# Two token blocks in alternation: a reordering inside the products by token of a two-layer encoder trunk on one Trainium2 core

## The chip, the cores and the metric

The kernel runs on one core of one Trainium2 chip. Four engines do the work that matters here. PE (TensorE) multiplies: a matmul reads a stationary operand of up to 128x128 and streams a moving operand past it, and it sums into a bank of PSUM (128 partitions x 512 floats). ACT (ScalarE) and DVE (VectorE) read and write SBUF and PSUM, and empty the banks. POOL (GpSimd) does almost nothing here. SP (SyncE) issues the loads and stores. Each engine works through its own queue strictly in order and waits on semaphores for what other engines produce.

The metric is the device time of one launch in microseconds (us). The kernel before was timed in three runs: the median is 1181.94 us, the lowest 1181.73 us, the highest 1183.77 us.

## The reference

The reference is a trunk of two layers over 512 tokens of width 1024, in fp32, with a memory of 256 tokens.

```
for i in range(DEPTH):                                   # DEPTH = 2
    h = rms_norm(x, attn_norm[i])
    if i % 2 == 0:  proj = h @ w_in_diff;  mix = diff_attention(q, k, v, ...)
    else:           proj = h @ w_in_gla;   mix = gla_attention(q, k, v, r, gate_low, ...)
    cross = memory_cross_attention(mem_q, mem, mem_norm[i], w_mem_kv[i], mem_qk_norm[i])
    x = x + concatenate([mix, cross]) @ w_out[i]
    h = rms_norm(x, ffn_norm[i])
    x = x + conv_ffn(h, w_up[i], conv_w[i], conv_b[i], w_down[i])
```

Layer 0 has differential attention with 6 heads: each head computes two softmaxes over 512 keys and subtracts them. Layer 1 has gated linear attention with 4 heads. In both layers 4 heads attend to the memory, whose keys and values are `rms_norm(mem) @ w_mem_kv[i]`, with one such product for each layer. The root mean square is taken over the whole width of a token, so its factor can be multiplied in after the product, one number for each token (row).

## The kernel before, in words

**Products.** Every fp32 product is made of three matmuls on operands that are split in a high and a low part: high x high, high x low and low x high. The weights arrive as raw fp32 tiles of 128x1024 by DMA (tile `raw`, three buffers). ACT casts each to its high part (`whi`, L205), and DVE subtracts to get the low part (`wlo`, L208); there are six buffers of each (`WB = 6`).

**Products by token.** `gemm` is the function that the change touches. A block of 128 tokens is the stationary operand, and the weights stream past it, up to 512 columns wide, so each block of tokens has its result in one bank of PSUM named `mm`, of which there are two. The inner width of 1024 is eight `k` of 128, and a unit of work is one block with two `k`: six matmuls. A weight tile of 128x1024 holds two `k` at 512 columns, so a unit uses one pair of tiles `whi`, `wlo`. With four blocks of tokens a `gemm` is 16 units; with the memory's 256 tokens it has two blocks and is 8 units. When a block has all eight `k`, `evac` empties its bank on ACT (two copies of 128x256 with a factor for each row, in most of them). `freed` is called by the last block after each `k`: when a pair of weight tiles has had its last use, it issues the cast and the subtraction of the next raw tile into the buffers and the load of a further one. Before the change block 0 takes all its `k`, then block 1, and so on.

Eleven calls of `gemm` are in the kernel. In layer 0: `vm0` (values of heads 0 and 1, and the memory queries), `qk1`, `kv0` (keys and values of the memory for layer 0), `v1`, `qk2` and `kv1` (the memory for layer 1). In layer 1: `gm1` (272 columns wide) and `g0` to `g4`. The two of the memory have `nb = 2`, the others `nb = 4`.

**The hook of kv0.** The memory's factor `r_mem` is computed by `token_rsqrt` (L370): four matmuls with a vector of ones (L373) sum the squares for each token into a bank `lg`, and then `rsqrt` runs Ln and Exp on ACT (L195, L196) and a Newton step on DVE (`newton`, L181 to L183). `gemm` calls this as its `hook` when block 0 has its last `k`, just ahead of the first `evac`. Only `kv0` and `gm1` have a hook; `kv1` reuses `r_mem`. Both evacuations of `kv0` (L499 for the keys, L500 for the values) multiply by `r_mem`.

**What sets the order.** PE's order is written out by hand. The units of `gemm` are put in a queue `F` (class `Filler`), and the attention of layer 0 goes through steps `t` = 0 to 20, each of which issues its own transposes, logits and value products and, between them, as many units of `F` as fit in a budget of microseconds (`FILL`, chosen with `STEPS`). A step has one unit of a head's attention: `logits(t)` (L650 on PE, L655 on DVE, L658 on ACT, L663 to L666 on DVE), `turn(t-1)` (transposes at L174, copied by ACT at L676) and `values(t-2)` (L688). `PREPARE` tells at which step a head's queries and keys are transposed (8 transposes into two banks `tp`, each copied by ACT at L617 to `qT` and `kT`); head `h` has its logits at steps 3h to 3h+2. `FINISH` tells at which step a head's output is transposed. The orders of ACT, DVE, POOL and SP are chosen by the framework's planner from the program's order and its own estimates of time.

**Layer 1** uses the same filler: the units of `g0` to `g4` run between the steps of the memory attention (L539 logits, L542 maximum, L546 exponential, L550 scaling, L559 copies) and of the gated heads (L926, L934). `g0` is emptied by two copies at L806, of 128x384 and 128x128.

The lines around the change stand in the kernel as follows.

Of the kernel before, what the change touches and what calls it, by code (L numbers as in the profile page):

```python
# [22 lines left out]
KT = D // 128  # L23
# [11 lines left out]

TOGETHER = ((2, 0), (1,), (3,))

PREPARE, FINISH = {5: 2, 7: 3, 11: 4, 13: 5}, {7: 0, 11: 1, 12: 2, 15: 3, 18: 4}
K8 = tuple(range(KT))
C4 = tuple(range(4))  # L40

# [92 lines left out]
def trunk(ctx, tc, head_d, x_t, mem_t, wpack, cols_a_d, cols_d, conv_d, gate_d, rel_bias, diff_lambda, consts, onehot, out):  # L134
# [12 lines left out]
    def bank(tag):  # L147
        return ps.tile([128, 512], F32, name=f"ps_{tag}", tag=tag)
# [12 lines left out]
    def blk(b, w=128):  # L161
        return slice(w * b, w * b + w)
# [84 lines left out]
    def weights(key, by_block=False):  # L247
        i = used[0]
        assert plan[i][0] == key, (plan[i][0], key)
        limit = first_of[i] + WB if by_block else first_of[min(i + 2, len(plan))]  # L250
        while done[0] < min(max(limit, first_of[i + 1]), len(order)):
            make_block()
        used[0] += 1
        parts, made[i] = made[i], None
        return parts

    def freed(i, k):
        if k in [sum(len(b[2]) for b in blocks[i][:j + 1]) - 1 for j in range(len(blocks[i]))] and done[0] < len(order):
            make_block()
# [6 lines left out]
    F = Filler()  # L266

    def gemm(sh, sl, nb, key, w, evac, hook=None):
        got, open_ = [], {}

        piece = [q[0] for q in plan].index(key)

        def unit(b, k0, k1):
            if not got:
                got.extend(weights(key, True))
            if k0 == 0:
                open_[b] = bank("mm")[:, :w]
            p = open_[b]
            for k in range(k0, k1):
                hi, lo = got[k]  # L280
                mm(p, sh[k][:, blk(b)], hi, start=k == 0, stop=False)  # L281
                mm(p, sh[k][:, blk(b)], lo, start=False, stop=False)  # L282
                mm(p, sl[k][:, blk(b)], hi, start=False, stop=k == KT - 1)  # L283
                if b == nb - 1:
                    freed(piece, k)
            if k1 == KT:
                if hook is not None and b == 0:
                    hook()
                evac(b, open_.pop(b))
        for b in range(nb):  # L290
            for k in range(0, KT, 2):
                F.add(6 * w / 2370.0, lambda b=b, k=k: unit(b, k, k + 2))


    def product(p, parts, n, pairs, ids=None):
# [90 lines left out]
    with tc.tile_pool(name="ini", bufs=1) as ip, tc.manual_schedule(engines={E.Activation, E.DVE, E.Pool, E.SP}):  # L386
# [53 lines left out]
        for k in range(KT):  # L440
# [22 lines left out]
            for b, i, t in todo:  # L463
                xp, w = terms[i]
# [18 lines left out]
    def mem_kv(l):  # L483
# [18 lines left out]
        def keys(tag="lg"):  # L502
            F.need(f"kv{l}")
            p = bank(tag)
            for hp in range(2):
                for b in range(2):
                    transpose(p[:, 256 * hp + 128 * b:256 * hp + 128 * b + 128], km[0][:, b, blk(hp)])
            A.activation(kmT[l].rearrange("p a b -> p (a b)"), p, AF.Copy, scale=c_mk(l))
        gemm(hs, ls, 2, ("kv", l), 512, ev,
             (lambda: token_rsqrt("lg", mem_acc[0], 2, r_mem)) if l == 0 else None)  # L510
        F.add(0.0, lambda: group_norm(None, km[0], 2, 4, 64))
# [68 lines left out]
    def diff_layer(pool, mix, acc):  # L580
# [16 lines left out]
        def project_qk(pr):  # L597
            qk[pr] = (pool.tile([128, NB, 256], F32, name="qs", bufs=1),
                      pool.tile([128, NB, 256], F32, name="ks", bufs=1))
            gemm(xh, xl, NB, ("qk", pr), 512, halves(*qk[pr]))  # L600
            F.mark(f"qk{pr}")
# [112 lines left out]
        norms(0, 0)  # L714
        norms(0, 1)
        gemm(xh, xl, NB, ("vm", 0), 512, halves(v0, qm))
        F.mark("v0")
        F.fill(10.0)
# [516 lines left out]
```

## Time and profile before

One launch was recorded by the hardware profiler.

| what | value |
|---|---|
| median of three runs | 1181.94 us (1181.73 to 1183.77) |
| time of the profiled launch | 1181.88 us |
| span of its instructions | 1180.1 us |
| granted TensorE clock | 1.00 |
| PE busy | 1168.3 us (99%) |
| DVE busy | 757.2 us (64%) |
| ACT busy | 547.0 us (46%) |
| DMA | 117.68 MB, mean 100 GB/s |

A launch is 1.8 us longer than its span. A line of the profile's tables gives an engine, an operation with its line in the kernel, the tile written and the tiles read without their buffer numbers, the shapes, and then times. In a timeline the first number is the start in us from the begin of the span and the second the duration; what stands in brackets is the idle time of that engine ahead of the instruction, and the instruction of another engine that ended it. In the table of waits a row reads: what waited, for what, the sum of the waits in us, how many there were, and the longest. Matmuls overlap in PE's pipeline: one of 128x512 is shown with 0.39 us, and the next starts 0.23 us after it.

### The profile page before, as it was taken

Reading aid. Unit: us, or ns where it says so; the run is one execution under the profiler, and the core shown is the slowest. Engines: PE = TensorE matmul, PEld = TensorE weight load, DVE = VectorE, ACT = ScalarE, POOL = GpSimd, SP = SyncE. Lnnn points to the kernel's source line nnn. Section 1 sums busy time; section 2 is a strip of 40 time slices with the busy share of each in tenths; the row PEclk is TensorE's granted clock in tenths of the full one; section 3 lists DMA queues with packets and bytes.
Section 4 is the critical chain, followed back from the end, with each engine's and each line's share of the span. In section 5 each row is a group of like instructions: output and inputs, shape, how many; then the busy total and the mean of one; then the engine's idle time right before and its main releaser. Section 6 shows DMA issues by size and latency. Waiting matters only on the chain.

```text
span 1180.1 us, 14805 instructions
## 1 busy us (share of the span) xinstructions
PE 1168.3 (99%) x5658; PEld 966.2 (82%) x5658; DVE 757.2 (64%) x1252; ACT 547.0 (46%) x952; POOL 4.6 (0%) x25
## 2 busy tenths in 40 slices
PE   9999999999999999999999999999999999999998
PEld 7887877888888888888888788988888888888887
DVE  7567677597767336677557646768777743476741
ACT  6676676465444213344437435436443422344420
POOL 0000000000000000000000000000000000000000
PEclk9999999999999999999999999999999999999999
DMA  8423214133323233223341221243232233232231
GB/s 287 141 93 95 76 59 130 59 125 107 108 72 108 89 107 104 93 81 107 118 145 55 72 72 58 68 143 125 72 116 98 77 121 107 71 124 74 75 113 44
DMA packets 39556, 117.68 MB, mean 100 GB/s; under 512 B 4703, under 2 KB 7192, under 8 KB 39486
## 3 DMA queue, kind: packets, MB, share of 16 engines
q1 hardware_dynamic: 39054, 116.35, 30.9%
q8 instruction: 44, 0.72, 0.3%
q10 hardware_dynamic: 432, 0.39, 0.1%
q14 instruction: 26, 0.21, 0.1%
HBM read 112.52 MB, written 4.21 MB: 99 GB/s over the span
## 4 chain that ended last, share of the span: by engine, by line
PE 92%; DVE 3%; ACT 3%; issue 1%; DMA 1%; SPq 0%; POOL 0%; DVEq 0%; ACTq 0%; POOLq 0%
PE ps_mm L300 9%; PE ps_mm L302 9%; PE ps_mm L301 9%; PE ps_sm L300 7%; PE ps_sm L301 7%; PE ps_sm L302 7%; PE ps_mm L281 5%; PE ps_mm L283 5%; PE ps_mm L282 5%; PE ps_lg L300 3%; PE ps_lg L301 3%; PE ps_lg L302 3%; PE ps_tp L300 3%; PE ps_tp L301 3%; PE ps_tp L302 3%; PE ps_tp L174 2%
## 5 line engine op out<-in xcount | busy, mean ns | idle before, releaser
L205 ACT CAST whi<-raw 128x1024 fp32r<-128x1024 f32 (+4 forms) x212 | 208.0, 986 | 247.7 <-PE ps_tp L301 120.9
L208 DVE TENSOR_TENSOR wlo<-raw,whi 128x1024 fp32r<-128x1024 f32 (+4 forms) x212 | 240.6, 1140 | 96.1 <-ACT whi L205 93.0
L300 PE MATMUL ps_mm<-xsh,whi 128*128 128x512 f32 x438 | 173.2, 395 | 0.5 <-ACT rr L806 0.5
L302 PE MATMUL ps_mm<-xsh,wlo 128*128 128x512 f32 x438 | 170.7, 390 | 0.0
L301 PE MATMUL ps_mm<-xsl,whi 128*128 128x512 f32 x438 | 170.5, 389 | 0.0
L300 PE MATMUL ps_sm<-xsh,whi 128*128 128x512 f32 x378 | 147.1, 389 | 0.0
L302 PE MATMUL ps_sm<-xsh,wlo 128*128 128x512 f32 x378 | 147.1, 389 | 0.0
L301 PE MATMUL ps_sm<-xsl,whi 128*128 128x512 f32 x378 | 147.0, 389 | 0.0
L281 PE MATMUL ps_mm<-whi,xsh 128*128 128x512 f32 (+2 forms) x352 | 136.3, 387 | 0.1
L283 PE MATMUL ps_mm<-whi,xsl 128*128 128x512 f32 (+2 forms) x352 | 131.0, 372 | 0.4 <-DVE xsl L263 0.4
L282 PE MATMUL ps_mm<-wlo,xsh 128*128 128x512 f32 (+2 forms) x352 | 130.6, 371 | 0.0
L1092 ACT ACTIVATE cvo<-u,cv 128x512 f32<-128x512 f32 x88 | 71.6, 815 | 123.5 <-DVE u L1090 123.5
L300 PEld LDWEIGHTS ps_mm<-xsh,whi 128*128 128x128 f32 x438 | 82.3, 188 | 17.7 <-ACT rr L806 0.9
L302 PEld LDWEIGHTS ps_mm<-xsh,wlo 128*128 128x128 f32 x438 | 82.2, 188 | 17.4
L301 PEld LDWEIGHTS ps_mm<-xsl,whi 128*128 128x128 f32 x438 | 82.3, 188 | 16.8 <-issue 0.5
L1093 DVE SCALAR_TENSOR_TENSOR cvo<-u,cv,cvo 128x512 f32<-128x512 f32 x88 | 65.8, 749 | 39.9 <-ACT cvo L1092 39.9
L302 PEld LDWEIGHTS ps_sm<-xsh,wlo 128*128 128x128 f32 x378 | 71.0, 188 | 14.8
L300 PEld LDWEIGHTS ps_sm<-xsh,whi 128*128 128x128 f32 x378 | 71.0, 188 | 14.7
L301 PEld LDWEIGHTS ps_sm<-xsl,whi 128*128 128x128 f32 x378 | 71.0, 188 | 14.6
L281 PEld LDWEIGHTS ps_mm<-whi,xsh 128*128 128x128 f32 x352 | 66.2, 188 | 13.6 <-issue 3.3
L283 PEld LDWEIGHTS ps_mm<-whi,xsl 128*128 128x128 f32 x352 | 66.1, 188 | 12.5 <-DVE xsl L263 0.6
L282 PEld LDWEIGHTS ps_mm<-wlo,xsh 128*128 128x128 f32 x352 | 66.3, 188 | 9.8
(273 smaller groups left out, 1744.5 us busy)
## 6 DMA issues: line engine op xcount, KB each, us to landing
raw<-in_wpack_dram SPq DMA_DIRECT2D x178, 512.0 KB, 3.5
xt<-in_x_t_dram SPq DMA_DIRECT2D x15, 256.0 KB, 5.2
raw<-in_wpack_dram SPq DMA_DIRECT2D x15, 256.0 KB, 3.2
raw<-in_wpack_dram SPq DMA_DIRECT2D x8, 384.0 KB, 3.2
xres<-xt SPq DMA_DIRECT2D x8, 256.0 KB, 3.2
xt<-xres SPq DMA_DIRECT2D x8, 256.0 KB, 4.5
out_dram<-xt SPq DMA_DIRECT2D x7, 256.0 KB, 2.0
bt<-bias_d SPq DMA_DIRECT2D x6, 256.0 KB, 4.5
```

Source lines behind the costliest of these rows:

```text
L174: nc.tensor.transpose(dst, src, ident[:n, :n])
L205: ins = A.copy(hi[:, c], raw[:, c])
L208: V.tensor_sub(lo[:, c], raw[:, c], hi[:, c].bitcast(F32))
L281: mm(p, sh[k][:, blk(b)], hi, start=k == 0, stop=False)
L282: mm(p, sh[k][:, blk(b)], lo, start=False, stop=False)
L283: mm(p, sl[k][:, blk(b)], hi, start=False, stop=k == KT - 1)
L300: mm(p, hi[:, blk(n)], bh, start=i == first, stop=False)
L301: mm(p, hi[:, blk(n)], bl, start=False, stop=False)
L302: mm(p, lo[:, blk(n)], bh, start=False, stop=i == last)
L1092: A.activation(c, u[:, 2:], AF.Identity, scale=cv[l][:, 2, j:j + 1], bias=cv[l][:, 3, j:j + 1])
L1093: V.scalar_tensor_tensor(c, u[:, 1:S + 1], cv[l][:, 1, j:j + 1], c, op0=ALU.mult, op1=ALU.add)
```

## The change

Two things change. In `gemm` the blocks of tokens except the last two run as they did. The last two, `nb - 2` and `nb - 1`, take turns: the first two `k` of the one, the first two `k` of the other, the next two `k` of the one, and so on. With four blocks the first half of a `gemm` stays as it was; with two blocks the whole of it alternates. Both banks `mm` are then open at the same time, and the two blocks end one unit apart. And the queries and keys of the last head (5) are transposed at step 14, not 13.

```
-PREPARE, FINISH = {5: 2, 7: 3, 11: 4, 13: 5}, {7: 0, 11: 1, 12: 2, 15: 3, 18: 4}
+PREPARE, FINISH = {5: 2, 7: 3, 11: 4, 14: 5}, {7: 0, 11: 1, 12: 2, 15: 3, 18: 4}
...
-        for b in range(nb):
-            for k in range(0, KT, 2):
-                F.add(6 * w / 2370.0, lambda b=b, k=k: unit(b, k, k + 2))
+
+        ks = range(0, KT, 2)
+        for b, k in [(b, k) for b in range(nb - 2) for k in ks] + [(b, k) for k in ks for b in (nb - 2, nb - 1)]:
+            F.add(6 * w / 2370.0, lambda b=b, k=k: unit(b, k, k + 2))
```

## The prediction

> **What bounds the kernel now.** I read the page's busy times, clock and chain first, since they tell which engine's time is the kernel's.
>
> ```profile
> PE 1168.3 (99%) x5658; PEld 966.2 (82%) x5658; DVE 757.2 (64%) x1252; ACT 547.0 (46%) x952; POOL 4.6 (0%) x25
> ...
> PEclk9999999999999999999999999999999999999999
> ...
> PE 92%; DVE 3%; ACT 3%; issue 1%; DMA 1%; SPq 0%; POOL 0%; DVEq 0%; ACTq 0%; POOLq 0%
> ```
>
> PE is busy for 1168.3 of 1180.1 us at full clock. The change removes no matmul and no byte, so it can only move PE's waits. The table of waits of PE, read next, holds all that can be regained:
>
> ```profile
> PE ps_tp L174 <- ACT xt L676: 2.1, 3, 1.0
> PE ps_tp L174 <- DVE xt L550: 1.6, 2, 1.3
> PE ps_tp L395 <- POOL idle L392: 1.3, 1, 1.3
> PE ps_lg L934 <- DVE xt L926: 0.9, 1, 0.9
> PE ps_lg L650 <- ACT kT L617: 0.8, 1, 0.8
> PE ps_mm L300 <- ACT rr L806: 0.5, 1, 0.5
> PE ps_mm L283 <- DVE xsl L263: 0.4, 1, 0.4
> PE ps_lg L650 <- ACT kmT L508: 0.4, 1, 0.4
> PE ps_sm L373 <- DVE xt L367: 0.2, 1, 0.2
> ```
>
> They add up to 8.2 us, 1.3 of it at the start. No row names an evacuated `mm` bank or a weight tile: today the products by token never wait for either. A gain is bounded by a few us; a loss is bounded only by what the alternation newly waits for. So I went through the timelines of PE, ACT and DVE with the changed order in hand, placing each unit at the time that its position has in the trace.
>
> **The change, part by part.**
>
> *1. Where alternation can cost.* With four blocks, a bank used to be refilled four units after its block ended. Now block 3 starts one unit after block 1 has ended, and the next product's first block starts one unit after block 2 has ended. A unit is 1.36 us (97.80 to 99.16, below) and an evacuation of two halves 0.85 us (0.37 between their starts plus 0.47), so it fits if ACT takes it at once, and is late by whatever stands ahead of it on ACT. For `vm0`, `qk1`, `v1`, `qk2`, `kv1` and `g1` to `g4` I find the evacuations done, or late by at most 0.1 to 0.2; ends for each 0 and one cast (1.03). I take 0.2 for all of layer 0 and 0.15 for layer 1, nearest to the former.
>
> The Trainium skill, "Perfetto Trace Analysis", section "Matmuls", says that independent groups should rotate through different PSUM banks so that the evacuation of one overlaps the matmuls of the next; two groups open at once use up both. It speaks against the change wherever ACT is late; no row of before shows such a wait, so it gives no price here.
>
> *2. kv0, the memory's product, two blocks.* Here alternation meets the hook:
>
> ```profile
> 91.08 0.50 PE L373 MATMUL ps_lg<-C,xt 128*128 128x1 f32 x4
> ...
> 97.80 0.39 PE L281 MATMUL ps_mm<-whi,xsh 128*128 128x512 f32 x1
> ...
> 98.94 0.39 PE L283 MATMUL ps_mm<-whi,xsl 128*128 128x512 f32 x1
> 99.16 0.39 PE L281 MATMUL ps_mm<-whi,xsh 128*128 128x512 f32 x1
> ...
> 102.98 0.66 PE L174 MATMUL ps_tp<-C,ks 128*128 128x128 f32 x4 [0.24 <-ACT xt L676]
> ```
>
> ```profile
> 95.60 0.48 ACT L499 ACTIVATE xt<-ps_mm,r_mem 128x256 f32<-128x256 f32 x1
> ...
> 100.38 1.03 ACT L205 CAST whi<-raw 128x1024 fp32r<-128x1024 f32 x1
> 101.32 0.47 ACT L499 ACTIVATE xt<-ps_mm,r_mem 128x256 f32<-128x256 f32 x1
> 101.69 0.46 ACT L500 ACTIVATE vm<-ps_mm,r_mem 128x256 f32<-128x256 f32 x1
> ```
>
> ```profile
> 95.41 0.15 DVE L183 SCALAR_TENSOR_TENSOR r_mem<-rs_t,r_mem 128x2 f32<-128x2 f32 x1
> ...
> 99.09 1.23 DVE L208 TENSOR_TENSOR wlo<-raw,whi 128x1024 fp32r<-128x1024 f32 x1
> ...
> 100.51 0.16 DVE L663 RECIPROCAL rcd<-smd 128x1 f32<-128x1 f32 x1
> ...
> 100.96 0.75 DVE L666 SCALAR_TENSOR_TENSOR xt<-xt,rcd 128x512 f32<-128x512 f32 x1
> ```
>
> Now the hook's four matmuls run at 91.08, `r_mem` is finished at 95.56, 4.5 us later, and block 0 is emptied from 95.60, while block 1 computes until 99.33; `v1` starts at 99.16 in the bank that block 0 left long ago. After the change block 0 ends one unit before block 1, so the hook moves 6.3 us later, to 97.34, and `v1` needs at once the bank whose evacuation needs `r_mem`. In the changed program ACT's queue has, ahead of Ln and Exp for `r_mem`, the cast into the tile that `kv0`'s very last matmul frees; DVE's has the subtraction of that tile, the reciprocals and L666 ahead of the last Newton operation. Worked out: last matmul ends at 98.94 + 0.39 = 99.33; cast 1.03 to 100.4; subtraction 1.23 to 101.6 (meanwhile ACT does L658, Ln and Exp); L663 and three small ones like it at 0.16 to 102.3; L666 0.75 to 103.0; L183 0.15; then two halves, 0.85, to 104.0. `v1` starts near 103.9 rather than 99.16: **+4.7 us**. Bounds: 0 if all were ready, and 6 if the hook's sums themselves come late (they need a bank `lg` that L655 releases, 0.2 to 0.3 us ahead of 97.34 by my placing). I take 4.7, since each link has a row. The wait of 0.24 at 102.98 goes, as ACT's copy is long done by then. Net +4.5. Queued behind on PE is everything, so nothing hides it.
>
> *3. Steps 12 to 15 of layer 0.*
>
> ```profile
> 172.59 0.66 PE L174 MATMUL ps_tp<-C,xt 128*128 128x128 f32 x4 [0.87 <-ACT xt L676]
> ...
> 183.00 1.14 PE L650 MATMUL ps_lg<-kT,qT 64*128 64x192 f32 x12 [0.77 <-ACT kT L617]
> ...
> 189.91 0.82 PE L688 MATMUL ps_sm<-v,xt 128*128 128x128 f32 x5
> ...
> 195.06 0.66 PE L174 MATMUL ps_tp<-C,ks 128*128 128x128 f32 x4 [1.03 <-ACT xt L676]
> ...
> 202.84 0.43 PE L650 MATMUL ps_lg<-kT,qT 64*128 64x192 f32 x2
> ```
>
> The casts of `qk2` and `kv1` spread over eight units rather than four, and ACT reaches the copy L676 earlier: the wait at 172.59 goes (-0.87; ends -0.87 and 0). `kT` of head 4 is still late at 183.00: 0. Head 5's eight transposes and two copies go past the products of one step, so the wait for the `tp` bank at 195.06 goes (-1.03); its `kT` is then due at 202.84, three matmuls at least after its transposes, and I see it in time (ends 0 and +0.77, the row where a `kT` was late). New: the values at 189.91 need a copy L676 that now stands behind a cast: +1.03, the cast's row at 100.38 (ends 0 and 1.03 + 0.85 for an evacuation as well). Net -0.9; the ends of the step are -2.5 and +1.
>
> SP is passed too: raw tiles are requested earlier and stand ahead of some loads of `x` and of the bias rows. No wait of PE names a DMA today; 0, with the one wait that shows in part 4 as price if that cover fails.
>
> *4. Layer 1.*
>
> ```profile
> 641.17 1.28 ACT L177 ACT_TABLE_LOAD   x1
> 642.46 0.37 ACT L806 ACTIVATE k<-ps_mm,r_x 128x128 f32<-128x128 f32 x1
> ...
> 652.59 2.95 ACT L205 CAST whi<-raw 128x1024 fp32r<-128x1024 f32 x3
> ...
> 688.27 1.05 ACT L205 CAST whi<-raw 128x1024 fp32r<-128x1024 f32 x1 [0.86 <-DMA raw<-in_wpack_dram]
> ```
>
> ```profile
> 641.47 0.50 PE L281 MATMUL ps_mm<-whi,xsh 128*128 128x512 f32 x1
> ...
> 661.10 0.63 PE L174 MATMUL ps_tp<-C,xt 128*128 128x128 f32 x4 [1.30 <-DVE xt L550]
> ...
> 692.43 1.16 PE L934 MATMUL ps_lg<-xt 96*128 96x128 f32 x8 [0.91 <-DVE xt L926]
> ```
>
> `g0`'s block 3 falls on the position at 641.47 and needs block 1's bank, whose second copy waits for a table load and ends at 642.46 + 0.37 = 642.83: +1.35 (ends 0 and 1.35). Against it, the three casts at 652.59, with their subtractions on DVE, run back to back today and make L550 late; alternated, `g0`'s tiles come free two units apart and partly before, so the waits of L550 go: -1.6 (ends -1.6 and 0). Likewise the late raw tile at 688.27 is requested earlier and the wait at 692.43 goes: -0.9 (ends -0.9 and 0). With 0.15 from part 1: -1.0.
>
> **Sum:** +0.2 + 4.5 - 0.9 - 1.0 = +2.8 on the profiled run's 1181.88, which stands 0.06 under the median: **1184.7 us**, 0.23% slower. A change under 0.2%, 2.4 us, can't be told from none in this kernel: slower is above 1184.3, faster below 1179.6.
>
> **The rivals.**
>
> *A: the earlier tiles give back more* (not slower). Place: steps 12 to 15. If the casts pass early enough that neither the copy for 189.91 (1.03) nor `kT` at 183.00 (0.77) is late, the time is 1184.7 - 1.8 = 1182.9. It decides from 0.4 us on. For it: ACT is busy only 46%. Against: the cast does stand ahead of that copy in the queue.
>
> *B: kv0's factor is not held up.* If neither the last cast (1.03) nor its subtraction (1.23) were in the way, `r_mem` would come 2.3 us earlier: 1182.4; with no wait at all 1180.2 (1184.7 - 4.5). For it: 4.5 us sufficed for the whole factor in the trace, among casts. Against: the queue orders above.
>
> *C: PE restarts cold after kv0.* The start of the trace shows the price:
>
> ```profile
> 5.42 1.05 PE L465 MATMUL ps_sm<-whi,xsh 128*128 128x512 f32 x2
> 6.28 0.95 PE L465 MATMUL ps_mm<-wlo,xsh 128*128 128x512 f32 x2
> 7.07 0.63 PE L465 MATMUL ps_sm<-wlo,xsh 128*128 128x512 f32 x2
> ```
>
> Two matmuls of 128x512 take 0.86 us (5.42 to 6.28), 0.43 each, where they later take 0.22 (98.94 to 99.16); this lasts until about 7, some 5.7 us after PE's first work at 1.3. Half of 5 us lost: 1184.7 + 2.5 = 1187.2. For it: 4.7 us idle, where the longest wait today is 1.3. Against: no gap inside this trace shows it. The Trainium skill, "TensorE: Matmul & The Clock Gate", section "Why this matters for your kernels", warns of gaps above about 3 us, after which the clock halves; its window runs freely, and by its 3.4 us a gap of 4.7 holds a whole one in (4.7 - 3.4) / 3.4, about four launches of ten (an estimate from that page). By the rows alone the case stays open, and I give it less than the other rivals together.
>
> *D: layer 1 gives nothing back.* If the casts only move to delay another L542 or L926, the waits of 2.5 us stay: 1184.7 + 2.5 = 1187.2. For it: both waits are ended by DVE, whose queue keeps the same subtractions. Against: the casts are spread, not added.
>
> **How the numbers follow.** My forecast 0.37 (its own range 1183.7 to 1185.7, most of it above 1184.3), A 0.25, B 0.11, C 0.14, D 0.13. Slower: 0.30 of the forecast's, C and D: 0.57. Within 0.2%: the rest of the forecast's, A, and about half of B: 0.37. Faster: 0.06. The range reaches from between B's two times, 1181.3, to a little past C and D, 1187.8; both together, or B without a wait, lie outside.
>
> **What would show it.** Right: in the waits of PE a row `mm` for a half of `kv0`'s evacuation (ACT, L500 of before) of 4 to 5 us near 99; L373 near 97.3; no wait of L676 at 172.6 and 195.1; one of about 1.3 at `g0`'s block 3; no wait of L550 and L926 near 661 and 692; the clock's row at 9 throughout. Wrong: no `mm` wait near 99 (B), matmuls 0.43 apart after it (C), or the waits for L550 and L926 still there (D).

## The result, and the profile after

The changed kernel takes 1187.78 us (median of 6 runs, 1186.17 to 1188.34) against 1181.84 us (6 runs, 1181.39 to 1183.77): a ratio of 1.0045 with a 95% interval of 1.0032 to 1.0058. It is slower, by 5.9 us.

The profiled launch took 1188.34 us. These are the page's lines for busy time, granted clock and chain; lines of the code from L290 on have moved down by one.

```profile
PE 1171.1 (99%) x5658; PEld 968.1 (82%) x5658; DVE 757.7 (64%) x1252; ACT 546.2 (46%) x952; POOL 4.6 (0%) x25
...
PEclk9998999999999999999999999999999999999999
...
PE 93%; DVE 3%; ACT 2%; DMA 2%; issue 0%; SPq 0%; DVEq 0%; ACTq 0%
```

PE's count of instructions is the same, and yet it is busy 2.8 us longer. The clock's row has an 8 in the fourth slice (89 to 119 us): there PE ran below full speed, which no slice of before shows. The waits of PE in the same launch:

```profile
PE ps_mm L281 <- ACT vm L501: 4.4, 1, 4.4
PE ps_mm L281 <- ACT k L807: 1.9, 1, 1.9
PE ps_sm L689 <- ACT xt L677: 1.3, 1, 1.3
PE ps_tp L396 <- POOL idle L393: 1.3, 1, 1.3
PE ps_lg L651 <- ACT kT L618: 0.7, 1, 0.7
...
PE ps_lg L348 <- DMA oh<-in_onehot_dram: 0.4, 1, 0.4
...
PE ps_mm L281 <- ACT qm L807: 0.2, 1, 0.2
PE ps_lg L935 <- DVE xt L927: 0.2, 1, 0.2
```

Three rows are new and large: a bank `mm` that waits for `kv0`'s evacuation (`vm`), one that waits for `g0`'s (`k`), and values that wait for a copy. The rows for L550 and L676 of before are gone, and L926 fell from 0.9 to 0.2.

The alternation permutes units of equal length, so PE's instruction number i can be compared between the two launches. The difference of their starts grows or shrinks only where PE waits more or less. Read at its steps:

| place (time of before) | what | change, us |
|---|---|---|
| first 17 us | the start: slow matmuls, a wait for `oh` | +0.7 |
| 71 | small delay in a product by token, not followed up | +0.15 |
| 99.16 | wait for `kv0`'s evacuation | +4.6 |
| 99.4 to 102 | PE at half clock | +2.5 |
| 102.98 | old wait gone | -0.45 |
| 172.59, 195.06 | old waits gone | -1.1, -1.1 |
| 189.91 | wait for L677 | +1.3 |
| 625, 635 | `g0`'s first block | +0.4, -0.25 |
| 641.47 | wait for `g0`'s `k` | +1.9 |
| 661, 662 | old waits gone | -1.55, -0.3 |
| 692.43 | old wait shorter | -0.8 |
| 736 | `g3`'s last block | +0.3 |
| 770 | next product's wait for `g4`'s evacuation (`rr`) | +0.15 |

The rows add up to +6.45 of the launch's 6.46 us. `kv0` in the changed kernel, PE, ACT and DVE in turn:

```profile
98.22 0.51 PE L374 MATMUL ps_lg<-C,xt 128*128 128x1 f32 x4
...
99.81 0.39 PE L283 MATMUL ps_mm<-whi,xsl 128*128 128x512 f32 x1
104.65 0.79 PE L281 MATMUL ps_mm<-whi,xsh 128*128 128x512 f32 x1 [4.45 <-ACT vm L501]
105.25 0.63 PE L282 MATMUL ps_mm<-wlo,xsh 128*128 128x512 f32 x1
105.67 0.63 PE L283 MATMUL ps_mm<-whi,xsl 128*128 128x512 f32 x1
```

```profile
100.24 1.04 ACT L205 CAST whi<-raw 128x1024 fp32r<-128x1024 f32 x1 [1.32 <-PE ps_mm L283]
101.19 0.72 ACT L659 ACTIVATE xt<-xt,nmd 128x512 f32<-128x512 f32 x1
...
101.91 0.24 ACT L195 ACTIVATE r_mem<-ps_lg,eps 128x2 f32<-128x2 f32 x1
...
103.76 0.47 ACT L500 ACTIVATE xt<-ps_mm,r_mem 128x256 f32<-128x256 f32 x1 [1.38 <-DVE r_mem L183]
104.13 0.47 ACT L501 ACTIVATE vm<-ps_mm,r_mem 128x256 f32<-128x256 f32 x1
```

```profile
101.32 1.22 DVE L208 TENSOR_TENSOR wlo<-raw,whi 128x1024 fp32r<-128x1024 f32 x1 [0.21 <-ACT whi L205]
...
102.91 0.75 DVE L667 SCALAR_TENSOR_TENSOR xt<-xt,rcd 128x512 f32<-128x512 f32 x1
103.57 0.15 DVE L183 SCALAR_TENSOR_TENSOR r_mem<-rs_t,r_mem 128x2 f32<-128x2 f32 x1
```

The chain is cast, subtraction, L667, L183, evacuation, in that order, and PE stands still from 100.2 to 104.65. Behind it the matmuls start 0.42 us apart (105.25 to 105.67), not 0.23. A table by stretches of the same launch gives the clock; after begin and end come the length, each engine's busy time with its count, and the granted TensorE clock:

```profile
99.57:102.98 3.41, 0.63 (x3) 0.19 (x1) 3.20 (x11) 2.11 (x5) 0.00 (x0) 1.00 0.52 174
102.98:106.39 3.41, 1.74 (x4) 1.45 (x5) 1.26 (x3) 2.08 (x5) 0.14 (x1) 0.50 0.58 178
106.39:109.81 3.42, 3.42 (x10) 2.64 (x10) 1.54 (x6) 0.88 (x3) 0.00 (x0) 0.50 0.00 1
109.81:113.22 3.41, 3.41 (x24) 2.91 (x25) 0.00 (x0) 1.27 (x2) 0.00 (x0) 1.00 0.00 0
```

The clock is exactly one half for two stretches of 3.41 us and full before and behind them. The third stretch has 10 matmuls and the fourth 24, though smaller ones are among the latter.

`g0` in the changed kernel, ACT and then PE:

```profile
648.41 1.28 ACT L177 ACT_TABLE_LOAD   x1
649.71 0.37 ACT L807 ACTIVATE k<-ps_mm,r_x 128x128 f32<-128x128 f32 x1
```

```profile
650.13 0.50 PE L281 MATMUL ps_mm<-whi,xsh 128*128 128x512 f32 x1 [1.93 <-ACT k L807]
```

The second half of block 1's evacuation stands behind the table load, as forecast, and ends at 650.08; block 3 starts right behind it. At 190 of before, 197 of after, ACT has these in front of the copy that the values wait for:

```profile
196.01 0.39 ACT L205 CAST whi<-raw 128x256 fp32r<-128x256 f32 x1
196.31 0.47 ACT L500 ACTIVATE xt<-ps_mm,r_mem 128x256 f32<-128x256 f32 x1
196.67 0.46 ACT L501 ACTIVATE vm<-ps_mm,r_mem 128x256 f32<-128x256 f32 x1
197.03 0.57 ACT L677 COPY xt<-ps_tp 128x512 f32<-128x512 f32 x1
```

### The profile page after: what moved, and what is told of

Read it like the earlier page. It is cut to its first block, busy times and chain, and to the rows that moved or that the text cites. A ratio compares the mean times of both kernels' runs of the same rounds, so it can differ in the third digit from the quotient of the medians.

```text
span 1186.6 us, 14812 instructions
## 1 busy us (share of the span) xinstructions
PE 1171.1 (99%) x5658; PEld 968.1 (82%) x5658; DVE 757.7 (64%) x1252; ACT 546.2 (46%) x952; POOL 4.6 (0%) x25
## 4 chain that ended last, share of the span: by engine, by line
PE 93%; DVE 3%; ACT 2%; DMA 2%; issue 0%; SPq 0%; DVEq 0%; ACTq 0%
PE ps_mm L301 9%; PE ps_mm L303 9%; PE ps_mm L302 9%; PE ps_sm L303 7%; PE ps_sm L302 7%; PE ps_sm L301 7%; PE ps_mm L281 6%; PE ps_mm L283 5%; PE ps_mm L282 5%; PE ps_lg L302 3%; PE ps_lg L303 3%; PE ps_lg L301 3%; PE ps_tp L302 3%; PE ps_tp L301 3%; PE ps_tp L303 3%; PE ps_tp L174 2%
```

## The experiments

All were run beside the kernel before, in three groups, each on one chip; in them the medians of before were 1181.41 (e1 to e4), 1181.58 (e5 to e8) and 1181.59 us (e9 to e11).

**e1: the memory's products in order.**

```
-        for b, k in [... for b in range(nb - 2) ...] + [(b, k) for k in ks for b in (nb - 2, nb - 1)]:
+        turns = nb > 2
+        tail = ([(b, k) for k in ks for b in (nb - 2, nb - 1)] if turns else
+                [(b, k) for b in (nb - 2, nb - 1) for k in ks])
+        for b, k in [... for b in range(nb - 2) ...] + tail:
```

> Edit: the changed kernel, but the two products of the memory (two blocks of tokens) run their blocks one after the other as before; the products with four blocks keep the alternation, and head 5 stays at step 14. Theory (the loss is kv0's late factor and the cold clock behind it): the wait of 4.4 us for vm near 100 us and the half clock behind it go together, 1187.8 - 4.7 - 2.5 = 1180.6 us, a little faster than before. Rival (the loss is the short time between a block's end and the next use of its bank, in every product alike): the four-block products keep their share and the time stays above 1185 us.

Measured: 1181.03 us (11 runs, 1179.21 to 1182.36), ratio 0.9993 [0.9984, 1.0002], no difference from before, so the small gain that was expected is not shown. The wait for `vm` and the half clock near 100 us are gone. The rival falls: the loss is not spread over all products. Against the whole change it is 6.75 us less, or 6.3 when each is taken against the kernel before of its own group, of the 7.2 expected.

**e5: kv0 alone alternates.** The kernel before, with `turns = key == ("kv", 0)`.

> Edit: the kernel before, with the alternation in kv0 alone (head 5 at step 13, all other products in order). Theory (kv0 alone carries the loss): a wait for vm of 4.4 us near 99 us and one or two windows of half clock behind it, 4.7 + 1.7 to 2.5 us on 1181.4: 1187.8 to 1188.6 us, slower than the whole change by the 1 us or so that its other parts give back. Rival (the wait needs the other products' shifted tiles and queues as well): under 1185 us.

Measured: 1189.2 us (6 runs, 1188.28 to 1190.88), ratio 1.0062 [1.0051, 1.0074]. That is more than the 1188.6 expected at most, but one product out of the twelve (six in each layer) carries the whole loss; whether it carries more than that, the two intervals, which overlap, don't show. Its trace shows the wait of 4.4 us again, and one more in front of it:

```profile
PE ps_mm L281 <- ACT vm L504: 4.4, 1, 4.4
...
PE ps_lg L377 <- DVE nmd L659: 0.9, 1, 0.9
```

The hook's sums (here L377) waited 0.9 us for a bank `lg` that DVE had not released: the second link that the prediction bounded at 6 us, absent in the whole change. This launch also has a window of half clock near 623 us, which cost 1.2 us; it lies 500 us behind `kv0`'s wait, and its cause is open.

**e2: the hook earlier.** The whole change, but `r_mem` is computed after block 0's second unit.

```
+            if hook is not None and b == 0 and k1 == (4 if nb == 2 else KT):
+                hook()
             if k1 == KT:
-                if hook is not None and b == 0:
-                    hook()
```

> Edit: the changed kernel, with the alternation everywhere, but in the two-block product the hook (squares of the memory summed, r_mem computed) runs after block 0's second unit instead of its last. Theory (the factor is late, not the bank): r_mem is ready before kv0 ends, both evacuations run at once, the wait in front of v1 is 0 to 0.5 us, the clock stays full, 1180.6 to 1181.2 us. Rival (bank reused one unit later is too early in any case, with a cast of 1.03 us and 0.85 us of evacuation in the way): a wait of 1 to 2 us stays, no cold clock, about 1182.5 us.

Measured: 1185.8 us (5 runs), ratio 1.0038 [1.0025, 1.0050]. Both numbers missed: a wait of 2.8 us stays, and the half clock with it. The factor is ready at 93.1, long before block 0 ends (DVE's last Newton operation, then ACT's timeline up to the evacuation):

```profile
92.95 0.16 DVE L183 SCALAR_TENSOR_TENSOR r_mem<-rs_t,r_mem 128x2 f32<-128x2 f32 x1
```

```profile
98.94 0.72 ACT L659 ACTIVATE xt<-xt,nmd 128x512 f32<-128x512 f32 x1 [3.24 <-DVE nmd L656]
...
99.66 1.03 ACT L205 CAST whi<-raw 128x1024 fp32r<-128x1024 f32 x1
100.69 0.72 ACT L659 ACTIVATE xt<-xt,nmd 128x512 f32<-128x512 f32 x1
...
101.41 0.45 ACT L500 ACTIVATE xt<-ps_mm,r_mem 128x256 f32<-128x256 f32 x1
101.77 0.46 ACT L501 ACTIVATE vm<-ps_mm,r_mem 128x256 f32<-128x256 f32 x1
```

Block 0's evacuation stands in ACT's queue behind the cast into the tile that block 1's last matmul frees, and behind two exponentials (L659), one on either side of that cast. So the order of the queue holds it, even with the factor at hand.

**e7 and e8: the cast behind the evacuation, without and with the early hook.** In both, the cast for the tile that `kv0`'s last matmul frees is kept behind what stands ahead of it in the program (block 0's evacuation).

```
-    split_weights(slice(0, n * w), raw, hi, lo, i == 2)
+    split_weights(slice(0, n * w), raw, hi, lo, pin or i == 2)
...
-            make_block()
+            make_block(pin=plan[i][0] == ("kv", 0) and k == KT - 1)
```

> Edit: the changed kernel, but the cast of the tile that kv0's last matmul frees is put behind block 0's evacuation in ACT's queue; the hook stays at the end of block 0. The early hook alone left 2.8 of the 4.4 us, so the factor's lateness is not all. Theory now (both hold it: the factor is late and the evacuation stands behind the cast): without the cast and its subtraction (1.03 and 1.23 us) in the way, but with the factor still behind L655 and L666, a wait of about 3 us, half clock for at least one window, 1185.5 to 1186.5 us. Rival (the order of ACT's queue is all): a wait under 1 us, 1181 to 1182 us.

> Edit: both together, the hook after block 0's second unit and the cast behind block 0's evacuation. Theory (late factor plus queue order make up the whole wait): block 0 is emptied right behind the exponential that waits for L655, a wait of 0.5 to 1.2 us, full clock there, 1181.0 to 1182.0 us. Rival (a third cause, such as the tiles of the next product or the bank itself): 2 us or more remain, 1183.5 us or more.

Measured: e7 1186.85 us (5 runs), ratio 1.0041 [1.0029, 1.0053]; e8 1182.73 us (12 runs, 1181.35 to 1183.15), ratio 1.0004 [0.9995, 1.0012], no difference from before. Their rows in the waits of PE:

```profile
PE ps_mm L281 <- ACT vm L501: 4.0, 1, 4.0
```

```profile
PE ps_mm L281 <- ACT vm L501: 1.0, 1, 1.0
```

ACT's timeline has block 0's evacuation and what it waited for, in e7 and then in e8:

```profile
99.57 0.72 ACT L659 ACTIVATE xt<-xt,nmd 128x512 f32<-128x512 f32 x1 [2.07 <-DVE nmd L656]
...
101.92 0.47 ACT L500 ACTIVATE xt<-ps_mm,r_mem 128x256 f32<-128x256 f32 x1 [1.16 <-DVE r_mem L183]
```

```profile
98.35 0.72 ACT L659 ACTIVATE xt<-xt,nmd 128x512 f32<-128x512 f32 x1 [3.24 <-DVE nmd L656]
...
99.07 0.45 ACT L500 ACTIVATE xt<-ps_mm,r_mem 128x256 f32<-128x256 f32 x1
```

The wait is 4.4 us with neither, 2.8 with the hook alone, 4.0 with the cast alone, and 1.0 with both. The cast alone is worth 0.4 because the factor is then the later of the two; only where both are removed does the wait go. e7's 3 us was too little: L667 and the exponential behind L656 stayed in the way. L656 itself runs behind two scalings of queries and keys on DVE (L340, 1.22 us each), which the prediction's chain does not have. What is left in front of the evacuation in e8 is an exponential that waits for L656 in the same way. e8's median lies above the range given; its trace has one stretch of half clock, now behind the wait of 1.9 us at `g0`, and the launches whose mean clock was 1.000 took 1181.35 to 1181.78.

**e4: PE kept busy through the wait.**

```
+        def keep_busy():
+            p = bank("tp")
+            for n in range(18):
+                mm(p, xh[0][:, blk(0)], xh[0], start=True, stop=True)
+        if l == 0:
+            F.add(0.0, keep_busy)
```

> Edit: the changed kernel with 18 more matmuls of 128x512 right behind kv0's last one, into a spare bank that nobody reads; they fill 18 x 0.227 = 4.1 us of PE's wait of 4.4 us. Theory (the gap turns the clock down, and half clock costs about 2.5 us): the wait shrinks to some 0.4 us, v1 starts at the same time, the clock stays full, 1187.8 - 2.5 = 1185.3 us. Rival (the half clock has another cause, or costs nothing on the path): no change, 1187.8 us; if the added matmuls come to lie on the path, up to 1190 us.

Measured: 1186.27 us (5 runs, 1185.17 to 1186.51), ratio 1.0039 [1.0025, 1.0053]. Its table by stretches, with the columns as above, first across `kv0`'s end and then around `g0`'s block 3:

```profile
99.50:104.00 4.50, 4.12 (x19) 3.10 (x18) 2.67 (x11) 3.08 (x10) 0.14 (x1) 1.00 0.57 181
643.26:646.67 3.41, 1.57 (x11) 0.89 (x10) 3.31 (x6) 3.22 (x6) 0.00 (x0) 1.00 0.03 5
646.67:650.09 3.42, 3.42 (x9) 2.65 (x9) 2.81 (x9) 2.68 (x10) 0.00 (x0) 0.50 0.00 0
```

The same chain with a busy PE: the clock stays full at `kv0` in this launch, and the median falls by 1.5 us (by 1.1 us when each is taken against the kernel before of its own group) although 18 useless matmuls were added. The intervals of the two kernels overlap, so the fall in time is not shown by itself; the trace shows that with PE busy the clock is not lowered there. So the idle time itself lowers the clock, and the steps read above show that the lowered clock costs on the path. The expected 1185.3 is about what the one launch with a mean clock of 1.000 took (1185.17); in the profiled one half clock came behind `g0`'s wait instead, and cost some 1.5 us there.

**e6: layer 1 alone alternates.** The kernel before with `turns = key[0] in ("gm", "g")`.

> Edit: the kernel before, with the alternation in the products of layer 1 alone (gm1, g0 to g4). Theory: the wait of 1.85 us for g0's k near 641 us, against 1.9 us regained for L550 near 661 and 0.8 us for L926 near 692, 0.4 us of small waits: -0.3 to -0.5 us as long as the clock holds, and up to +1.7 us more in those launches where the wait of 1.85 us brings one window of half clock (3.4 us long), so a median of 1181 to 1182.5 us. Rival (layer 1 gains clearly, as my sum of -1.0 us had it): 1180.4 us or less.

Measured: 1182.16 us (11 runs, 1181.33 to 1183.47), ratio 1.0002 [0.9993, 1.0010]. Layer 1 gains nothing that can be measured. The profiled launch, at full clock, is 0.5 us ahead at the end, but only 0.15 of that arises in layer 1. Five of the eleven launches have a mean clock under 1.000 and took 1182.33 us or more; that `g0`'s wait lowered it in them is likely but not shown, since only one launch was recorded. The rival, my own sum, falls.

**e11: layer 1 without g0.** `turns = key[0] in ("gm", "g") and key != ("g", 0)`.

> Edit: the kernel before with one-unit alternation in gm1 and g1 to g4 only; g0 in order, head 5 at step 13. Theory (g0's own alternation both takes the 1.9 us near 641 and gives the 1.9 us near 661): neither a wait for k near 641 nor a gain for L550 near 661; the 0.8 us at L926 near 692, which belong to g1, stay: 1181.0 us, all launches at full clock there. Rival (the tiles that L550 gains from are gm1's, or the 692 gain is g0's): L550's waits go too, 1179.5 us, or nothing moves, 1181.6 us.

Measured: 1181.43 us (11 runs), ratio 0.9998 [0.9989, 1.0006]. Both waits of L550 near 661 are back (1.6 us, as before), the wait for `k` at 641 is gone, and the gain near 692 stays (-0.8). So it is `g0`'s own alternation that takes 1.9 us at one place and gives 1.9 back at the other.

**e3: head 5 at step 14, nothing else.**

> Edit: the kernel before with only head 5's transposes moved from step 13 to step 14. Theory: the wait of 1.03 us at 195.06 goes and nothing takes its place, 1181.9 - 1.0 = 1180.9 us. Rival (the wait only moves to head 5's kT at step 15, 0.77 us as head 4's at 183.00, or to a copy behind it): 1181.6 to 1182.2 us.

Measured: 1181.23 us (11 runs), ratio 0.9999 [0.9991, 1.0008]; the profiled launch has -0.7 us at 195 and -0.15 at 172, and no other change. The theory holds in the trace, where L676's waits fell from 2.1 to 1.2 us; the time can't tell 0.8 us from none.

**e9 and e10: the last block two units behind.** e9 is the whole change with the memory's products in order; e10 alternates in layer 1 alone, with head 5 at step 14. In both the last block follows the last but one by two units.

```
+        tail = ([(b, k) for j in range(len(ks) + 1)
+                 for b, k in ((nb - 2, 2 * j), (nb - 1, 2 * j - 2)) if k in ks] if turns else
+                [(b, k) for b in (nb - 2, nb - 1) for k in ks])
```

> Edit: the changed kernel, the memory's products in order, and in the four-block products the last block follows two units behind the last but one, not one (so block 1's bank has two units, 2.7 us, to be emptied). Theory (one unit is too short a time where ACT is late): the wait of 1.85 us for g0's k shrinks to about 0.5 us and with it the launches with half clock near 641 us go, the other gains of layer 1 stay: from 1181.0 (one unit, memory in order) to 1178.5 to 1179.5 us. Rival (the later last block frees the tiles later again, so L550 waits near 661 us as before): 1180 us or more.

> Edit: the kernel before with head 5 at step 14 and, in layer 1's products alone, the last block two units behind the last but one. Theory (layer 0's alternation gives 1.1 us near 172 and takes 1.3 us at 190, nothing net): as the other kernel of this call within 0.5 us, 1178.5 to 1179.8 us. Rival (layer 0's alternation gains by itself): 1 us or more slower than the other.

Measured: e9 1179.28 us (11 runs, 1178.74 to 1181.16), ratio 0.9983 [0.9974, 0.9992]; e10 1179.67 us (11 runs, 1179.36 to 1180.07), ratio 0.9979 [0.9970, 0.9988]. Both are faster than before, by 0.2%, and both lie in the range that was expected. No row for a bank `mm` on a product by token is left in e9's waits of PE, and part of L550's (here L554) has come back. The product right behind layer 1's products by token now waits 0.8 us for a bank `mm` (L304, for DVE's L1046) where it waited 0.5 us before:

```profile
PE ps_mm L304 <- DVE xt L1046: 0.8, 1, 0.8
...
PE ps_tp L174 <- ACT xt L680: 0.7, 3, 0.3
PE ps_tp L174 <- DVE xt L554: 0.6, 2, 0.3
```

One more unit of distance took the whole 1.9 us at 641 and left more than half of what the earlier tiles gave. Layer 0's alternation adds nothing that can be measured (e9 against e10: 0.4 us).

## Why the prediction was right, and where it was not

The forecast was slower, at 1184.7 us; it came out slower, at 1187.78. The direction and the cause at `kv0` were right. The size was not: the forecast's own range ended at 1185.7, and the median lies inside the whole range by 0.02 us only because that was drawn out to the rivals C and D, which is luck. The parts, with the launch's numbers:

- **kv0's wait (+4.7): right**, in place and size (4.6), and every link that it named stands in the trace. But the working followed one chain to its end and called every link a price. The runs show two conditions that hold the evacuation in parallel, the late factor and the cast ahead of it in ACT's queue; rival B, which took the cast and the subtraction out for 2.3 us, would have gained 0.4 (e7).
- **The old wait at 102.98** went, -0.45 for -0.24: the bracket of a row showed less than the delay.
- **Half clock: the step that failed.** Rival C had it at 2.5 us and a chance of 0.14; it was there in size (2.5) and place. e4's trace shows the mechanism. The sum had nothing for it: I priced the loss at full clock although the trace's start had matmuls 0.43 us apart, and argued that no gap inside the trace showed it; but no wait of before was longer than 1.3 us, so the trace could not speak against it. All six launches of the changed kernel have a mean clock under 1.000 (0.997 to 0.999). Forecast plus C is 1187.2. The Trainium skill, "TensorE: Matmul & The Clock Gate", section "What's actually happening", gives a free-running window of 3413 ns, and the two stretches of 3.41 us agree.
- **Steps 12 to 15 (-0.9): right**, by -1.1, -1.1 and +1.3 with 0 at `kT`. The copy behind 189.91 was held by an evacuation and a short cast (1.3), not by a long cast (1.03).
- **Layer 1 (-1.0): too much.** The launch has -0.2. The waits of L550 and L926 went as said (-1.85 for -1.6, and -0.8 for -0.9), but `g0`'s block 3 waited 1.9 us, not 1.35: ACT's queue had reached the table load later, at 648.41, against PE's place at 648.2, and I had taken its time from before. Rival D, nothing given back, was wrong in its reason, yet e6 shows its result: nothing measurable is left of layer 1's gain.
- **Part 1 (+0.2 in layer 0)** fits the +0.15 near 71, whose cause was not followed up.
- **Two readings** were wrong without weight in the sum. The table of waits of before does have a row for a bank `mm` that waits for an evacuation (L300 for `rr`, 0.5 us), at the product behind `g4`. And the ends of the step for steps 12 to 15, -2.5 and +1, are not what the ends of its terms add up to (-1.9 and +1.6).
- **Rivals A and B** did not come: `kT` was still late by 0.7 and the values by 1.3; the wait at `kv0` was whole.
- **The start (+0.7)** was not in the sum; it varies between launches (-0.8 to +0.7 against before's profiled one) and is no part of the change.

## What to carry to other kernels

When two accumulations share the only two banks, look for the first thing that has to empty one of them soon, and list everything that stands ahead of that evacuation: its scale factor and, separately, its place in the engine's queue; both have to be right. With the memory's products left in order, a distance of two units in place of one gave a gain of 0.2% (e9) where none could be measured with one unit (e1), though the two intervals overlap. And price a long wait of PE with what follows it, not only with its length.

## What the runs showed of the hardware that was not expected

A gap need not fill a window to halve the clock. I laid windows of 3.41 us, counted from the first change of the clock, over the traces of all thirteen kernels, and summed PE's busy time in each. Away from the ends of the launches, six windows at full clock held only 0.13 to 1.57 us of work, and each was followed by a window of half clock: behind `kv0` 0.63 us in the changed kernel, 0.69 in e2, 0.13 in e5 and 0.96 in e7, and at `g0` 1.57 in e4 and 1.47 in e8. Of the windows between 1.76 us and three quarters none was. e6 gives the other side, with much the same wait as e4 (1.9 us, and 1.8 in e4) on another place of the grid:

```profile
638.08:641.49 3.41, 3.13 (x18) 2.06 (x16) 2.11 (x5) 3.33 (x8) 0.00 (x0) 1.00 0.00 0
641.49:644.90 3.41, 1.76 (x8) 1.46 (x9) 3.29 (x7) 2.49 (x7) 0.00 (x0) 1.00 0.02 5
644.90:648.32 3.42, 3.42 (x17) 2.84 (x16) 2.84 (x5) 3.03 (x8) 0.00 (x0) 1.00 0.00 0
```

At the ends of the launches seven windows with 0.09 to 1.33 us of work were followed by half clock too, but one with 1.56 us was not (the changed kernel, from 1181.59). So the border lies a little under half a window, near 1.6 us of work. The traces place it no closer, since the ends of matmuls in them are modelled. Whether a wait of 1.9 us costs 1.9 or 3.5 us depends on where it falls. A wait of 4.45 us, as at `kv0`, leaves at least one window with 1.2 us of work or less, wherever it falls (an estimate: 3.41 less half of 4.45); by that the half clock had to come there. Once at half clock, 1.74 and 1.87 us of work (the changed kernel, e7) did not bring the clock back; a full window did. The Trainium skill, "TensorE: Matmul & The Clock Gate", section "What's actually happening", speaks of an idle window after which the clock halves; here a window with 46% of work in it was enough (e4).

Two things stay open. One window of half clock in e5, near 623 us, stood behind a window in which PE was busy for over three quarters. And the kernel before, which has no such wait, has a mean clock under 1.000 in 13 of its 71 launches of the three groups (1181.77 to 1185.35 us). So that e1, e6 and e8, which keep the wait at `g0`, spread over 2 to 3 us where e10 spreads over 0.7 is not shown to come from that wait: e3 and e11 spread as widely without it.
